# Two ConvFFNs and their surroundings: norms beside the GLU, four products ahead, copies in another room, w_out two tiles behind

## The chip, the cores and the metric

The kernel runs on one core of a Trainium2 chip, as one launch. The metric is the device time in microseconds (us), as the median of three runs. The engines named below are PE (TensorE, the matmul engine), DVE (VectorE), ACT (ScalarE), POOL (GpSimd) and SP (SyncE, which here issues nearly all DMAs; its DMA queue is written SPq). Each engine works through its own list of instructions in order, and waits at semaphores for the others.

## The reference

A backbone block of depth 2 over 1024 latent tokens and 256 context tokens, width 1024. Layer 0 mixes tokens by an S5 state-space layer and a GLU, layer 1 by a matrix-memory LSTM (mLSTM) with four heads. Each is followed by a gated ConvFFN of inner width 2816 (22 tiles of 128). In layer 1 only the latent tokens are carried on.

```python
def _conv_ffn(h, w_in, conv_w, w_out):
    u = _dwconv(h @ w_in, conv_w)                 # 3 taps along the tokens
    a, g = jnp.split(u, 2, axis=-1)
    return (a * jax.nn.silu(g)) @ w_out
...
    y = jax.nn.gelu(...)                          # end of the S5 mixer
    a, g = jnp.split(y @ glu_w + glu_b, 2, axis=-1)
    return a * jax.nn.sigmoid(g)
...
    proj = hf @ w_in                              # mLSTM: q, k, v, o
    ... heads(proj[..., 2 * D:3 * D]), jax.nn.sigmoid(proj[..., 3 * D:])
...
for i in range(2):                                # the block
    x = x + g1 * y_lat;   ctx = ctx + cg1 * y_ctx            # mixer
    x = x + g2 * _conv_ffn(_rmsnorm(x, norm2_g[i]) * (1 + sc2) + sh2, w_in[i], conv[i], w_out[i])
    ctx = ctx + cg2 * _conv_ffn(...)                         # layer 0 only
return _rmsnorm(x, final_g)
```

## The kernel before, in words

Activations lie with channels on the 128 partitions (8 groups k of 128) and tokens along the free axis. Every fp32 operand of a matmul is split into a high and a low part (`split`, L195 on ACT writes the high part, L196 on DVE the low one), and a product is the sum of three matmuls. Weights come by SP's DMAs into raw slots `wr`, are split into a ring of five slots `s`, and are read from there.

The program runs in stages: S5; GLU of the latent tokens (tile `u`, 8 steps m of two halves); GLU of the context (`uc`, L376, 384 matmuls of 256 columns) with norm 2 of layer 0 between; FFN 0 of the latent tokens (`ffn_wide`, L560); its output product; FFN 0 of the context (`ffn_ctx`: `uf` L376, `cacc` L452); mLSTM (v products with the gates L1319, q, k and o products L344); norm 2 of layer 1; FFN 1 (`ffn_wide` again); final norm.

`ffn_wide` does its input product as Strassen's seven products (numbered 1 to 7) per tile f. A product is 12 matmuls of 512 columns into one PSUM tile (`bA`, `bB` or `bC`). The seven need different forms of the normed activations. Products 1 and 2 need only `B11` and `B21`, which are plain splits (`h` or `he`). Products 6, 5, 7 and 4 need sums and differences (`T1` to `T4`, `B22`; L491 to L503, `hl` and `he`), which DVE builds in place and splits. The weights of products 5, 6, 7 and of two others are sums of raw weights (L544), split in the same ring. A copy (L570) keeps product 1 in a room `s13`; in layer 1 that room lies in row 0 of `x`.

A norm (`Norm`) takes squares (ACT L251), adds them up (L254), sums over partitions by one-column matmuls (`columns`, `nps` L271), takes a reciprocal root in some ten to fourteen tiny instructions (`nv`, `ni`, `nt`, `nr`, L204 to L223, on POOL or DVE) and spreads it over partitions by transposes (`spread`, `nps` L286). Then DVE multiplies (`plain`, `nm` L299). Before FFN 0 there are four norms of 256 columns on POOL.

In `ffn_ctx` step f computes `uf` of tile f, then the output product `cacc` of tile f-1, whose `gh` and `gl` come from the convolution and the gate on ACT and DVE (L460 to L465).

From the context GLU on, PE's order is the order in which the code is written (`manual_schedule`). The order on DVE, ACT, POOL and SP is set by a scheduler's estimate.

Of the kernel before, what the change touches and what calls it, by code (L numbers as in the profile page):

```python
# [425 lines left out]
def ffn_ctx(e, ins, x, H, ring, raws, accs, ubank, gp, beside):  # L426
# [6 lines left out]
    prev = None  # L433
    for f in range(FT + 1):
# [19 lines left out]
        if f < FT:
# [11 lines left out]
            prev = [gp.tile([128, 256], F32R, name=f"g{q}") for q in "hl"]  # L466
            split(nc, *prev, ts[1])
# [41 lines left out]
def ffn_wide(e, ins, layer, F, ring, raws, sums, scr, psum, gd, halves, first):

# [20 lines left out]
    def loads(f):  # L531
        for n, (k, m) in {"A11": (0, f), "A21": (0, f + FT), "A12": (4, f), "A22": (4, f + FT)}.items():
# [719 lines left out]
def mlstm(e, ins, x, xpool, npool, wpool, ahead, left, H, T, hpool):  # L1252
# [219 lines left out]
    def in_proj(h, kinds, passes=BOTH, pools=((wp, 2),), tp=tp):  # L1472

        pools = cycle(pools)
        for kind in kinds:
# [6 lines left out]
            for j in range(2):  # L1482
# [3 lines left out]
                for p in passes if kind == "k" else BOTH[1:]:  # L1486
# [352 lines left out]
def tile_hybrid_block(ctx: ExitStack, tc: tile.TileContext, ins, out):  # L1839
# [37 lines left out]
    with ExitStack() as zrc:
        zrp = zrc.enter_context(tc.tile_pool(name="gzr", bufs=2, reuse_waits="tile"))
        z = glu_tokens(e, x, yscr, zl, zc, zrp)
        for m in range(KT):  # L1880
            us = []
            for half in (1, 0):
                u = pu.tile([128, 2, 512], F32, name="u", tag="u")
                mm_halves(nc, [u[:, b] for b in range(2)], half_weights(e, ring, raws, w, m + 8 * half),
                          lambda k, b, part: z[0][part][:, k, 4 * b:4 * b + 4].rearrange("p i c -> p (i c)"))
                us.append(u)
                if m == 0 and half:
                    glu_residual(e, ins, x, zrp, po)
            glu_gate(e, x, m, us, NCH - NCC, 0, sp)
# [23 lines left out]
    def park0(j):  # L1913
        c = LAT0 + 256 * j
        nc.sync.dma_start(xd[0][:, :, 256 * j:256 * j + 256], x[:, :, c:c + 256])

    def plain0(j):
# [327 lines left out]
```

## Time and profile before

| | us |
|---|---|
| median of 3 runs | 3103.88 (3098.01 to 3104.23) |
| profiled execution, its time | 3099.47 |
| its span | 3097.4 |
| PE busy | 2790.1 (90%) |
| DVE busy | 2143.1 (69%) |
| ACT busy | 1409.3 (45%) |
| POOL busy | 341.7 (11%) |

The span is one profiled execution; its own time is 2.07 us above the span. A row of a timeline is: start, duration, engine, line, operation, output from input, count, and in brackets the idle time before it with what released it. Durations of neighbouring matmuls overlap in the record, so the pace is the distance of starts. Times in the text are on the span's axis.

### The profile page before, as it was taken

Reading aid. Unit: us, or ns where it says so; the run is one execution under the profiler, and the core shown is the slowest. Engines: PE = TensorE matmul, PEld = TensorE weight load, DVE = VectorE, ACT = ScalarE, POOL = GpSimd, SP = SyncE. Lnnn points to the kernel's source line nnn. Section 1 sums busy time; section 2 is a strip of 40 time slices with the busy share of each in tenths; the row PEclk is TensorE's granted clock in tenths of the full one; section 3 lists DMA queues with packets and bytes.
Section 4 is the critical chain, followed back from the end, with each engine's and each line's share of the span. In section 5 each row is a group of like instructions: output and inputs, shape, how many; then the busy total and the mean of one; then the engine's idle time right before and its main releaser. Section 6 shows DMA issues by size and latency. Waiting matters only on the chain.

```text
span 3097.4 us, 44668 instructions
## 1 busy us (share of the span) xinstructions
PE 2790.1 (90%) x16336; PEld 2376.3 (77%) x16336; DVE 2143.1 (69%) x4049; ACT 1409.3 (45%) x2579; POOL 341.7 (11%) x523
## 2 busy tenths in 40 slices
PE   4875399988999999999999899999887999999999
PEld 2561067877788887888998899999876788887877
DVE  6789943359777775437774978878777777777352
ACT  5650413246444454335653344545545444445342
POOL 5440000031000000002001121211112000000011
PEclk9885599999999999999999999999998999999999
DMA  8348536142222226446543443343532122226540
GB/s 227 107 89 255 160 73 203 48 130 86 82 82 82 82 91 205 147 146 202 161 119 98 128 147 127 123 136 99 188 92 69 63 81 82 82 82 216 175 150 28
DMA packets 418187, 382.52 MB, mean 123 GB/s; under 512 B 48248, under 2 KB 348064, under 8 KB 415664
## 3 DMA queue, kind: packets, MB, share of 16 engines
q1 hardware_dynamic: 417632, 379.56, 39.5%
q8 instruction: 128, 2.10, 0.3%
q14 instruction: 91, 0.75, 0.1%
q10 hardware_dynamic: 336, 0.12, 0.0%
HBM read 311.44 MB, written 68.16 MB: 123 GB/s over the span
## 4 chain that ended last, share of the span: by engine, by line
PE 70%; DVE 16%; issue 7%; ACT 3%; DMA 2%; POOL 2%; SPq 1%; DVEq 0%; POOLq 0%; ACTq 0%
PE bA L560 16%; PE acc L639 11%; PE bC L560 8%; PE u L344 6%; PE u L376 6%; PE bB L560 4%; PE uf L376 3%; PE u L1319 3%; PE ou L1536 2%; PE py L1213 2%; PE cacc L452 2%; PE po L1536 2%; DVE X L1191 2%; DVE tmp_v L1188 2%; DVE tmp_v L1190 1%
## 5 line engine op out<-in xcount | busy, mean ns | idle before, releaser
L196 DVE TENSOR_TENSOR s<-wr,s 128x512 fp32r<-128x512 f32 x545 | 377.4, 696 | 375.7 <-ACT s L195 371.7
L195 ACT ACTIVATE s<-wr 128x512 fp32r<-128x512 f32 x545 | 341.3, 631 | 640.7 <-PE bA L560 214.6
L560 PE MATMUL bA<-h,s 128*128 128x512 f32 x1056 | 261.4, 402 | 20.6 <-ACT x L570 14.8
L560 PEld LDWEIGHTS bA<-h,s 128*128 128x128 f32 x1056 | 201.9, 192 | 71.4 <-ACT x L570 15.0
L344 PE MATMUL u<-h,wh 128*128 128x258 f32 (+1 forms) x1184 | 231.5, 284 | 4.1 <-DVE s L1501 2.9
L254 POOL TENSOR_TENSOR nacc<-nacc,nsq 128x256 f32<-128x256 f32 (+1 forms) x96 | 85.7, 904 | 1231.3 <-ACT nsq L251 1219.4
L344 PEld LDWEIGHTS u<-h,wh 128*128 128x128 f32 x1184 | 182.7, 190 | 5.1 <-ACT wh L195 4.3
L344 PE MATMUL u<-h,wl 128*128 128x258 f32 (+1 forms) x640 | 152.5, 284 | 4.5 <-DVE wl L196 4.5
L376 PE MATMUL u<-zh,s 128*128 128x512 f32 x512 | 140.4, 395 | 11.9 <-ACT s L195 11.9
L560 PE MATMUL bA<-he,s 128*128 128x512 f32 x528 | 131.8, 399 | 9.0 <-ACT s L195 6.2
L196 DVE TENSOR_TENSOR h<-wr,h 128x512 fp32r<-128x512 f32 x107 | 71.0, 690 | 89.5 <-ACT h L195 84.9
L639 PE MATMUL acc<-h 128*128 128x512 f32 (+1 forms) x564 | 131.4, 373 | 0.0
L560 PE MATMUL bA<-hl,s 128*128 128x512 f32 x528 | 130.5, 395 | 0.0
L560 PE MATMUL bC<-h,s 128*128 128x512 f32 x528 | 128.3, 398 | 0.0
L560 PEld LDWEIGHTS bA<-he,s 128*128 128x128 f32 x528 | 101.0, 192 | 32.7 <-ACT s L195 6.6
L196 DVE TENSOR_TENSOR m<-wr,m 128x512 fp32r<-128x512 f32 x116 | 79.5, 698 | 65.9 <-ACT m L195 64.4
L544 DVE TENSOR_TENSOR wr<-wr 128x512 f32<-128x512 f32 x176 | 121.8, 694 | 2.7
L376 PEld LDWEIGHTS u<-zh,s 128*128 128x128 f32 x512 | 97.2, 191 | 32.4 <-ACT s L195 12.4
L595 DVE SCALAR_TENSOR_TENSOR x<-x,conv 128x1023 f32<-128x1023 f32 x88 | 112.8, 1282 | 13.3 <-ACT x L594 13.3
L155 PE MATMUL ada<-adaw,csil 128*32 128x256 f32 x560 | 70.6, 602 | 56.9 <-DMA adaw<-in_ada_w_dram 56.9
L639 PE MATMUL acc<-s,s 128*128 128x512 f32 x480 | 115.3, 394 | 6.7 <-DVE s L196 4.6
L560 PEld LDWEIGHTS bC<-h,s 128*128 128x128 f32 x528 | 100.1, 190 | 24.5
(519 smaller groups left out, 7269.1 us busy)
## 6 DMA issues: line engine op xcount, KB each, us to landing
wr<-in_ffn_w_in_dram SPq DMA_DIRECT2D x264, 256.0 KB, 3.0
wr<-in_ffn_w_out_dram SPq DMA_DIRECT2D x220, 256.0 KB, 3.1
adaw<-in_ada_w_dram SPq DMA_DIRECT2D x70, 512.0 KB, 5.2
gd<-x SPq DMA_DIRECT2D x44, 512.0 KB, 2.6
wr<-gd SPq DMA_DIRECT2D x88, 256.0 KB, 3.5
wraw<-in_ml_w_in_dram SPq DMA_DIRECT2D x44, 512.0 KB, 4.4
wr<-in_s_glu_w_dram SPq DMA_DIRECT2D x64, 256.0 KB, 2.9
X<-in_ada_w_dram SPq DMA_DIRECT2D x26, 512.0 KB, 4.8
```

The lines of the kernel that those rows point to most:

```text
L155: nc.tensor.matmul(acc[32 * q:32 * q + 32, h * n:h * n + n], lhsT=e.csil[:, k, :], rhs=wt[:, q, :], start=(k == 0 and h == 0), stop=(k == ...
L195: nc.scalar.activation(hi, src, AF.Copy)
L196: nc.vector.tensor_sub(lo, src, f32(hi))
L254: eng.tensor_add(self.acc, self.acc, sq)
L344: nc.tensor.matmul(outs[b], lhsT=w[:, k, :], rhs=rhs(k, b, part), start=i == 0, stop=i == n - 1)
L376: nc.tensor.matmul(o, lhsT=w, rhs=rhs(k, b, part), start=k + i == 0, stop=(k, i) == (KT - 1, 2), skip_group_check=True)
L544: nc.vector.tensor_tensor(R[n, f], R[x, f], R[y, f], op=op)
L560: nc.tensor.matmul(out, lhsT=w[:, k * 128:(k + 1) * 128], rhs=F(part, b, k), start=first and n == 0, stop=n == 11, skip_group_check=True)
L595: nc.vector.scalar_tensor_tensor(t[:, 1:], u[:, i, :-1], cw[0], t[:, 1:], op0=OP.mult, op1=OP.add)
L639: nc.tensor.matmul(out[:, a:a + n], lhsT=w, rhs=g[:, a:a + n], start=k == 0 and i == 0, stop=k == FT - 1 and i == 2, skip_group_check=True)
L1319: nc.tensor.matmul(at[t], lhsT=H[b](hp, k)[:, 1 + 128 * t:129 + 128 * t], rhs=w[wq][:, k % 4], start=k == 0 and j == 0, stop=k == KT - 1 a ...
L1536: nc.tensor.matmul(out, lhsT=w, rhs=r, start=i + j == 0, stop=(i, j) == (len(terms) - 1, 2))
```

## The change

The latent GLU loop now takes the squares of two norms of 512 columns and parks `x` in DRAM, step by step. Their adds and roots are on DVE. `columns` comes after the first half of the first `uc` product, `spread` after the second, and what follows (`plain`, splits, forms) is dealt out six pieces to each further `uc` step. `ffn_wide` starts with products 1 and 2 of tiles 0 and 1 in both layers; the tile-1 loads `A21`, `A22` come after tile 0's sums. `forms_b` begins with `T3` and `T4` of k = 0. In layer 1 `s13` lies in `wr[10]`, `wr[11]`, there are 6 raw slots in place of 8, the third norm's root is on DVE, and its `spread` and `plain` are written after the first two products. `ffn_ctx` does `w_out` two tiles behind. The o product of head 0 for blocks 1 and 2 (96 matmuls, tile `uo`) is moved from the mLSTM to the end of `ffn_ctx`, and its result goes out by the DMA `od<-so`. The pools of one region stand in another order (`ss`, `wr`, then the slots).

```diff
-    prev = None
-    for f in range(FT + 1):
+    prev = deque()
+    for f in range(FT + 2):
...
-        if prev:
+        if f > 1:
...
-                nc.sync.dma_start(t, w_out[(f - 1) * 128:f * 128, q * 512:(q + 1) * 512])
+                nc.sync.dma_start(t, w_out[(f - 2) * 128:(f - 1) * 128, q * 512:(q + 1) * 512])
...
-            gh, gl = prev
+            gh, gl = prev.popleft()
...
-            prev = [gp.tile([128, 256], F32R, name=f"g{q}") for q in "hl"]
+            prev.append([gp.tile([128, 256], F32R, name=f"g{q}", bufs=3) for q in "hl"])
...
+    for fs, ks in (((t3, t4), (0,)), ((t3,), (1, 2, 3)), ((t4,), (1, 2, 3)), ((b22,), range(4))):
+        for k in ks:
+            for f in fs:
+                f(k)
...
-    order = [(p, f) for f in range(first) for p in (1, 2)]
-    for f in range(FT):
-        order += [(1, f)] * (f >= first) + [(4, f - 1), (3, f - 1)] * (f > 0)
-        order += [(5, f), (6, f), (2, f), (7, f)] if f >= first else [(6, f), (5, f), (7, f)]
+    order = [(1, 0), (2, 0), (1, 1), (2, 1), (6, 0), (5, 0), (7, 0), (4, 0), (3, 0), (6, 1), (5, 1), (7, 1)]
+    for f in range(2, FT):
+        order += [(1, f), (4, f - 1), (3, f - 1), (5, f), (6, f), (2, f), (7, f)]
...
+            if f == 0:
+                loads(1, ("A21", "A22"))
+            elif f < FT - 1:
                 loads(f + 1)
...
-                for p in passes if kind == "k" else BOTH[1:]:
+                for p in passes if kind == "k" else BOTH[2:] if kind == "o" and h == 0 else BOTH[1:]:
...
+    ss = wp.tile([128, 2, 512], F32, name="ss")
+    wr = wp.tile([128, 10, 512], F32, name="wr")
     slots = [wp.tile([128, 2, 512], F32R, name=f"s{i}") for i in range(5)]
-    wr = wp.tile([128, 10, 512], F32, name="wr")
-    ss = wp.tile([128, 2, 512], F32, name="ss")
...
-    n0 = [Norm(e, npool, po, x, LAT0 + 256 * b, 256, "C") for b in range(4)]
...
+                n0 = [Norm(e, gn, po, x, LAT0 + 512 * b, 512, "C", nc.vector, nc.vector, nt=1) for b in range(2)]
+        glu_gate(e, x, m, us, NCH - NCC, 0, sp)
+        for n in n0:
+            n.square(m)
+        nc.sync.dma_start(xd[0][:, m], x[:, m, LAT0:LAT0 + SEQ])
...
-                if m in (0, 1, 2, 3):
-                    n0[m].columns()
-                if m in (1, 2, 3, 4):
-                    plain0(m - 1)
-                if m in (1, 2):
-                    n0[m + 1].squares()
-                    park0(m + 1)
+            if m == 0:
+                for n in n0:
+                    n.columns() if half else n.spread()
+        for _ in range(6 if m else 0):
+            next(steps0, None)
...
+    for j in range(2):
+        us = [pu.tile([128, 512], F32, name="uo", tag=t)[:, :256] for t in "CC"]
+        mm_halves(nc, us, half_weights(e, ring, raws, ins["ml_w_in"][0], 24 + j), lambda k, b, part: H1(b + 1)(part, k)[:, 1:257])
+        s = gp.tile([128, 2, 256], F32, name="so")
+        for b in range(2):
+            nc.scalar.activation(s[:, b], us[b], AF.Tanh, scale=0.5)
+        nc.vector.tensor_scalar(s, s, 0.5, 0.5, op0=OP.mult, op1=OP.add)
+        nc.sync.dma_start(e.od[0, :, j, 0:512], s.rearrange("p b n -> p (b n)"))
...
-    n1 = [Norm(e, npool, pu, x, LAT0 + 256 * b, 256, "C", nc.vector if b == 3 else None, nc.vector if b == 3 else None, nt=3) for b in B1]
+    n1 = [Norm(e, npool, pu, x, LAT0 + 256 * b, 256, "C", nc.vector if b == 3 else None, nc.vector if b in (0, 3) else None, nt=3) for b in B1]
...
-    n1[2].spread()
-    plain(2)
...
-           Ring([xf[:, 0:512], xf[:, 512:1024]]), ss[:, 0])
+           Ring([wr[:, 10], wr[:, 11]]), ss[:, 0])
...
-    raws, sums = Ring([wr[:, i] for i in range(8)]), Ring([wr[:, i] for i in range(8, 12)])
+    raws, sums = Ring([wr[:, i] for i in range(6)]), Ring([wr[:, i] for i in range(6, 10)])
...
         if n == 2:
+            n1[2].spread()
+            plain(2)
             n1[3].columns()
```

On PE, at the start of FFN 0, the first products stood like this (`bA`, `bB`, `bC` are the PSUM tiles; products 1, 2, 6, 5, 7 of tile 0, then 1 of tile 1):

```order
L560 MATMUL bA<-he,s_3388 128x512 x12
L560 MATMUL bB<-he,s_3384 128x512 x12
L560 MATMUL bA<-he,s_3385 128x512 x12
L560 MATMUL bC<-he,s_3386 128x512 x12
L560 MATMUL bA<-hl,s_3387 128x512 x12
L560 MATMUL bA<-he,s_3388 128x512 x12
```

and stand now like this:

```order
L567 MATMUL bA<-he,s_3390 128x512 x12
L567 MATMUL bB<-he,s_3386 128x512 x12
L567 MATMUL bA<-he,s_3387 128x512 x12
L567 MATMUL bB<-he,s_3388 128x512 x12
L567 MATMUL bA<-he,s_3389 128x512 x12
L567 MATMUL bC<-he,s_3390 128x512 x12
L567 MATMUL bA<-hl,s_3386 128x512 x12
```

Products 1 and 2 of tile 1 (third and fourth row) stand ahead of product 6 of tile 0, which was third.

On DVE, shortly before that product 6 can be complete, the changed program has these rows (`he<-x` in the last row but one is the low part of the last piece of `T2`, which product 6 reads; `hl` are pieces of other forms):

```order
L504 TENSOR_TENSOR x<-x 128x512
L492 TENSOR_TENSOR x<-x,ss 128x512
L500 TENSOR_TENSOR x<-x 128x512
L196 TENSOR_TENSOR he<-x,he 128x512
L196 TENSOR_TENSOR hl<-x,hl 128x512 x5
L549 TENSOR_TENSOR wr<-wr 128x512
L196 TENSOR_TENSOR hl<-x,hl 128x512 x3
L504 TENSOR_TENSOR x<-x 128x512
L196 TENSOR_TENSOR hl<-x,hl 128x512 x2
L196 TENSOR_TENSOR he<-x,he 128x512
L196 TENSOR_TENSOR hl<-x,hl 128x512
```

Ten `hl` splits stand ahead of that last piece of `T2`.

On SP's DMA queue, from the end of `ffn_ctx` into the mLSTM, the rows before were:

```order
L445 DMA wr<-in_ffn_w_out_dram 128x512 x4
L1338 DMA gb<-in_ml_b_if_dram 128x2x4 x2
L1301 DMA wraw<-in_ml_w_in_dram 128x4x256
L1304 DMA wraw<-in_ml_w_if_dram 128x4x4 x4
L1301 DMA wraw<-in_ml_w_in_dram 128x4x256
L1304 DMA wraw<-in_ml_w_if_dram 128x4x4 x4
```

and are now:

```order
L445 DMA wr<-in_ffn_w_out_dram 128x512 x6
L363 DMA wr<-in_ml_w_in_dram 128x4x128 x4
L1307 DMA wraw<-in_ml_w_in_dram 128x4x256
L1310 DMA wraw<-in_ml_w_if_dram 128x4x4 x2
L2053 DMA od<-so 128x512
L1310 DMA wraw<-in_ml_w_if_dram 128x4x4 x2
L1307 DMA wraw<-in_ml_w_in_dram 128x4x256
L1310 DMA wraw<-in_ml_w_if_dram 128x4x4 x4
```

The store `od<-so` stands between the loads of the first v weights, with six small gate loads and one large load behind it.

## Rows read from the trace of the kernel before

**Rows 1.** Stretches: us, busy and instructions of PE, PEld, DVE, ACT, POOL; PEclk; DMA:

```profile
500.00:550.00 50.00, 50.00 (x261) 42.24 (x260) 15.48 (x23) 14.35 (x24) 0.00 (x0) 1.00 0.40 132
684.00:756.00 72.00, 57.33 (x358) 51.20 (x358) 70.23 (x130) 48.44 (x99) 20.75 (x26) 0.88 0.39 110
1690.00:1760.00 70.00, 63.23 (x521) 61.76 (x520) 66.98 (x118) 23.72 (x33) 10.11 (x7) 0.96 0.30 93
```

**Rows 2.** Waits of PE, 655 to 800 us: total, times, longest:

```profile
PE nps L286 <- POOL nr L223: 8.3, 2, 5.7
```

**Rows 3.** Timeline of PE, context GLU and first products of FFN 0:

```profile
664.31 0.36 PE L376 MATMUL uc<-zh,s 128*128 128x256 f32 x1
...
670.00 0.50 PE L271 MATMUL nps<-ones,nacc 128*128 128x1 f32 x4
...
728.88 2.98 PE L560 MATMUL bB<-he,s 128*128 128x512 f32 x12
738.04 1.22 PE L560 MATMUL bA<-he,s 128*128 128x512 f32 x2 [6.18 <-ACT s L195]
741.56 3.86 PE L560 MATMUL bA<-he,s 128*128 128x512 f32 x10 [2.29 <-DVE s L196]
745.26 1.08 PE L560 MATMUL bC<-he,s 128*128 128x512 f32 x4
```

**Rows 4.** Timeline of DVE, the splits before FFN 0:

```profile
743.83 4.29 DVE L196 TENSOR_TENSOR hl<-x,hl 128x512 fp32r<-128x512 f32 x7
```

**Rows 5.** Waits of PE, 1400 to 1640 us:

```profile
PE cacc L452 <- ACT gh L195: 11.6, 5, 3.1
PE u L1319 <- ACT wh L195: 6.7, 1, 6.7
PE cacc L452 <- DVE gl L196: 3.4, 5, 1.2
```

**Rows 6.** Timeline of PE, context FFN and first v products:

```profile
1425.87 0.38 PE L452 MATMUL cacc<-gl,m 128*128 128x256 f32 x1 [0.71 <-DVE gl L196]
...
1429.80 0.41 PE L452 MATMUL cacc<-gh,m 128*128 128x256 f32 x1
...
1623.62 0.39 PE L452 MATMUL cacc<-gl,s 128*128 128x256 f32 x1 [0.23 <-DVE gl L196]
...
1634.51 0.82 PE L1319 MATMUL u<-wh,h 128*128 128x272 f32 x2 [6.71 <-ACT wh L195]
...
1639.17 0.41 PE L1319 MATMUL u<-wh,h 128*128 128x272 f32 x2
```

**Rows 7.** SP's DMA queue after the last cacc matmul:

```profile
1627.84 0.37 SPq L1301 DMA_DIRECT2D wraw<-in_ml_w_in_dram  x1
1628.25 2.29 SPq L1304 DMA_DIRECT2D wraw<-in_ml_w_if_dram  x4
```

**Rows 8.** DMA issues, 1615 to 1645 us: count, KB, us to landing:

```profile
wraw<-in_ml_w_if_dram SPq DMA_DIRECT2D x8, 8.0 KB, 2.9
```

**Rows 9.** Timeline of ACT, first split of v weights:

```profile
1633.36 1.09 ACT L195 ACTIVATE wh<-wraw 128x1088 fp32r<-128x1088 f32 x1
```

**Rows 10.** Timeline of DVE, start of the mLSTM's gate chain:

```profile
1691.75 0.41 DVE L1399 COPY gi<-pt 4x256 f32<-4x256 f32 x1 [4.94 <-PE pt L1396]
```

**Rows 11.** Timeline of PE, first products of FFN 1:

```profile
2366.47 0.69 PE L286 MATMUL nps<-kc,nr 128*128 128x128 f32 x2 [7.85 <-POOL nr L223]
2366.82 5.47 PE L560 MATMUL bA<-h,s 128*128 128x512 f32 x12
...
2406.44 1.22 PE L560 MATMUL bA<-h,s 128*128 128x512 f32 x2 [0.76 <-DVE h L196]
2407.45 4.16 PE L560 MATMUL bC<-h,s 128*128 128x512 f32 x12
```

**Rows 12.** Timeline of DVE, third norm's root and forms of layer 1:

```profile
2377.47 0.16 DVE L210 SCALAR_TENSOR_TENSOR nt<-nt,nv 128x2 f32<-128x2 f32 x1
...
2381.49 1.26 DVE L299 SCALAR_TENSOR_TENSOR nm<-x,gain,nps 128x256 f32<-128x256 f32 x3 [1.61 <-PE nps L286]
```

More of the change, by code (lines that the diff above doesn't have):

```diff
@@ L529, in half, with loads @@
         return half_of(t, 0, halves[i])
-    def loads(f):
-        for n, (k, m) in {"A11": (0, f), "A21": (0, f + FT), "A12": (4, f), "A22": (4, f + FT)}.items():
+    def loads(f, names=("A11", "A21", "A12", "A22")):
+        for n in names:
+            k, m = 4 * (n[2] == "2"), f + FT * (n[1] == "2")
             R[n, f] = raws()
@@ L600, in gated @@
         nc.sync.dma_start(gd[f], tg)
-    for f in range(first):
-        loads(f)
+    loads(0)
+    loads(1, ("A11", "A12"))
     ahead = len(ring.items)
-    late = 2 * first if first > 1 else 0
     for n in range(ahead - 1):
@@ L611, in ffn_wide @@
         yield n
-        if n == late:
-            for i in order[:late]:
+        if n == 4:
+            for i in order[:4]:
                 combine(*i)
         product(p, f)
-        if n >= late:
+        if n >= 4:
             combine(p, f)
@@ L1875, in tile_hybrid_block @@
     halves = (0, 1), (2, 3)
-    n0 = [Norm(e, npool, po, x, LAT0 + 256 * b, 256, "C") for b in range(4)]
[L1877 to L1889, printed above, removed]
+    zrc = ExitStack()
+    zrp = zrc.enter_context(tc.tile_pool(name="gzr", bufs=2, reuse_waits="tile"))
+    z = glu_tokens(e, x, yscr, zl, zc, zrp)
+    for m in range(KT):
+        us = []
+        for half in (1, 0):
+            u = pu.tile([128, 2, 512], F32, name="u", tag="u")
+            mm_halves(nc, [u[:, b] for b in range(2)], half_weights(e, ring, raws, w, m + 8 * half),
+                      lambda k, b, part: z[0][part][:, k, 4 * b:4 * b + 4].rearrange("p i c -> p (i c)"))
+            us.append(u)
+            if m == 0 and half:
+                glu_residual(e, ins, x, zrp, po)
+                zrc.close()
+                gn = gc.enter_context(tc.tile_pool(name="gn", bufs=1, side="right", reuse_waits="tile"))
+                n0 = [Norm(e, gn, po, x, LAT0 + 512 * b, 512, "C", nc.vector, nc.vector, nt=1) for b in range(2)]
[3 more added lines that the diff above has]
+        nc.sync.dma_start(xd[0][:, m], x[:, m, LAT0:LAT0 + SEQ])
     lc.close()
@@ L1911, in blocks0, with steps0 @@
         return half_of(x, k * NCOL + LAT0, halves[i])
[L1913 to L1917, printed above, removed]
-        c = LAT0 + 256 * j
-        n0[j].spread()
-        n0[j].plain(lambda k: x[:, k, c:c + 256], 0, 1)
-        if j == 1:
-            for k in range(4):
-                for f, kk in ((B11, k), (B21, k + 4)):
-                    split(nc, two(F0(0, f, k)), two(F0(1, f, k)), blocks0(kk, 0))
+    def steps0():
+        for j in range(2):
+            c = LAT0 + 512 * j
+            for k in range(KT):
+                n0[j].plain(lambda k: x[:, k, c:c + 512], 0, 1, (k,))
+                yield
+                if not j and k > 3:
+                    for f, kk in ((B11, k - 4), (B21, k)):
+                        split(nc, two(F0(0, f, k - 4)), two(F0(1, f, k - 4)), blocks0(kk, 0))
+                        yield
+        for k in range(4):
+            forms_a(nc, F0, k, blocks0(k, 0), blocks0(k, 1), blocks0(k + 4, 1), two(ss[:, k % 2]))
+            for _ in range(4):
+                yield
+    steps0 = steps0()
     order = ExitStack()
     order.enter_context(tc.manual_schedule(engines={nc.tensor.engine}))
-    for j in range(2):
-        n0[j].squares()
-        park0(j)
     for m in range(KT):
@@ L1969, in tile_hybrid_block @@
     load, mm, add = ffn_out(e, ins, 0, x, gd[0], ring, raws)
-    for n in ffn_wide(e, ins, 0, F0, ring, raws, sums, scr, bank0, gd[0], halves, 1):
+    for n in ffn_wide(e, ins, 0, F0, ring, raws, sums, scr, bank0, gd[0], halves):
         if n == 10:
```

31 lines of the change are left out of this document (15 added, 16 removed).

## The prediction, made blind

> **What bounds the kernel now.** I read the page first: PE is busy 90% of the span, so a gain must come from the places where PE stands. The table of stretches of 50 us shows those places, the list of PE's waits names them, and the timelines of PE, DVE and SP tell what came last. Four places matter for this change.
>
> First, the context GLU and the start of FFN 0. PE waits for roots on POOL [rows 2], and then for DVE: from 684 to 756 us DVE is busy 70.23 of 72 us while PE is busy 57.33 [rows 1]. Product 6 waits 6.18 and 2.29 us, and product 5 begins at 745.26 with only three products behind it [rows 3]. Second, the context FFN: `cacc` waits 11.6 us for `gh` and 3.4 for `gl`, in five places each [rows 5]. Third, the step into the mLSTM: after the last `cacc` matmul SP issues the v weights at 1627.84 and PE is at its pace again at 1639.17 [rows 6, 7]. Fourth, the start of FFN 1: 7.85 us for a root on POOL, then a DVE chain from 2381.49 to the last wait of product 6 at 2406.44 [rows 11, 12]. During the latent GLU, by contrast, PE is full and DVE is busy 15.48 of 50 us [rows 1].
>
> **Latent GLU: norms and parking.** Added per step are two squares on ACT, two adds on DVE (512 columns, 0.61 each, from seven splits in 4.29 us [rows 4]) and one store. DVE and ACT have over 34 us in 50 free there [rows 1], and PE works from a ring of five slots. I cost it at nothing; if that cover fails it is the slow rival below.
>
> **Context GLU and first products, layer 0.** `columns` still ends when it did, at 664.3 [rows 3]. The two roots are then 24 tiny DVE instructions. One is busy 0.16 [rows 12]; I take 0.2 from start to start, an estimate, and one split between: `spread` at 669.7. The POOL wait of 5.7 us [rows 2] goes. What is late next is DVE. In its new order, from the first `nm` to the last `T2` piece, there stand 107 instructions of about 0.61 us (16 `nm` of 512 columns, which have no row and are priced as splits of that width, 59 splits, 16 steps of the forms, 8 weight sums, 8 gate products) and 9 short ones, at an estimate of 0.4: 65.3 + 3.6 = 68.9. That puts the last `T2` piece at 738.6; with 1.4 for waits I take 740. PE meanwhile has 336 `uc` matmuls at 0.1185 (48 of them between 664.31 and 670.00 [rows 3]), 39.8 us, and four products of 2.8 (12 matmuls, bB in 2.98 with its tail [rows 3]), and is ready for product 6 by about 721. So product 5 begins at 740 + 1.0 (the same two matmuls took 1.0 in layer 1, 2406.44 to 2407.45 [rows 11]) = 741 with five products behind it, against 745.3 with three: 4.3 + 2 x 2.8 = 9.9. Product 5 itself comes out of a long wait. In layer 1, after such a wait, it took 4.16 [rows 11] against 2.8, so 1.4 is given back: 8.5 us. Lower bound: the ten `hl` splits and the sums hold `T2` until 745, which leaves 3.5. Upper bound: the ten `hl` splits fall into waits, 6.1 earlier, 15.
>
> The change gathers several short waits into one long one, and the mean granted clock of 684 to 756 was 0.88 [rows 1], a mix of the levels 1.2 and 2.4 GHz. The Trainium skill ("TensorE: Matmul & The Clock Gate", Part 1: The HAM clock gate) says that the throttled state is the default and activity releases it, which speaks against gathering the waits. The 4.16 of layer 1 agrees. By the rule product 7 could be slow too, and the gain then 7.1 instead of 8.5.
>
> **Context FFN, `w_out` two tiles behind.** Before, one `cacc` of 24 and one `uf` of 48 matmuls lie between the end of `uf(f)` and `cacc(f)`: 72 x 0.1185 = 8.5 us. Now it is twice that, 17. The waits are at most 3.1 and 1.2 us long [rows 5], so the chain through convolution, gate and split needs up to about 12.5, and is covered. Of 15.0 us of waits the last place (3.1 + 0.2) belongs to the next part: 11.7. After a wait `cacc` runs slower: the 22 intervals from 1425.87 to 1429.80 took 3.93 [rows 6] against 2.6 at 0.1185, so 1.3 more at each of four places. Together 16.9. I take 14.5, as DVE and ACT stay as full as they were and the weight splits, now earlier against the gates, can come last once or twice. Bounds 8 and 17. A third `g` buffer keeps the writer from waiting.
>
> **Into the mLSTM.** Before, the loss is 3.3 for the last `gh`/`gl`, 1.5 for slow matmuls (1623.62 to the end at 1627.8, 4.2 instead of 2.7), and 1627.8 to 1639.17 less the 12 matmuls done in it, 11.4 - 1.6 = 9.8: 14.6 in all [rows 6]. Now `cacc` is followed by 96 matmuls `uo`, 11.4 us, and the v weights no longer share a room with the slots, so the first large load goes out early. But the store `od<-so` stands in SP's order ahead of two of the first half's gate loads and of the whole second half. It waits for the first half of `uo`: 5.7 + about 1.3 for tanh and scaling (estimate) = 7.0 after the last `cacc`. Then two gate loads at 0.57 (four in 2.29 [rows 7]), 2.9 to land [rows 8], 1.1 for the split [rows 9]: 12.2, against PE's 11.4. The second half comes after another 0.4 + 2.3 of issuing: 14.9, where PE would want it at 13.7. With the low parts behind the high ones the residue is about 3, and 0.5 for the clock: gain 14.6 - 3.5 = 11. Bounds: no residue, 14.6; all eight small loads and one more split late, 6, so 8.6.
>
> The Trainium skill ("DMA: Bandwidth & Descriptors", Anatomy of one DMA) says that DMA engines do not wait on semaphores, the issuing sequencer does, before dispatch. That speaks against this store in this queue. Rows 7, where the gate loads go out one by one behind the first load, agree with an ordered queue. Were the store not in the way the gain would be 14, by the rule it is the 11 above.
>
> **The o product's move.** It costs 11.4 us before the mLSTM and saves 11.4 inside, if PE's work is what bounds there. From 1690 to 1760 DVE is busy 66.98 of 70 us [rows 1], so PE's work would be worth nothing there, unless that DVE chain starts earlier too. It does: DVE stood idle 4.94 us for the transposes `pt` [rows 10], and in PE's order 99 matmuls of L344 stand ahead of these, 192 before: 93 fewer, 11.0 us. So I take 0; bounds -11.4 (chain held by its inputs) and +3 (two more loads of weights and their splits now lie in a covered place).
>
> **Layer 1.** The third norm's nm no longer stand between the plain splits in DVE's queue, where DVE stood until the root on POOL came [rows 11]. Product 1 of tile 0 then runs with the splits (it took 5.47 at a slow clock [rows 11]), and the four products end about 5 us earlier. The fourth norm's root now queues behind a weight split, so its `spread` moves from 2381.1 to about 2377.5 (estimate): 3.6. The chain of DVE from there to the last `T2` piece was 25.0 us [rows 11, 12]; two instructions fewer, 1.2. Sum 4.8, say 5; bounds 1 (the queue is full anyhow) and 10. `s13` in another room frees ACT's copies, but DVE's chain ends last there, so that is worth nothing by itself.
>
> **Sum.** 8.5 + 14.5 + 11 + 0 + 5 = 39. The profiled execution took 3099.47 (span 3097.4 and 2.07 around it), so it would take 3060.5. The median lies 4.4 above that execution, so 3065.
>
> **Rivals.**
> A, DVE binds: DVE and ACT set both FFN starts, and fewer waits of PE only lengthen others. For: 70.23 of 72. Against: the roots on POOL left DVE idle too. Layer 0 gives 3.5, layer 1 gives 1: 3074.
> B, the o product is not given back: the gate chain's inputs come no earlier. For: DVE's 66.98 of 70. Against: the 4.94 idle for PE. 11.4 worse: 3076.
> C, the change does not do what it says in the context FFN: the waits are named for `gh`, but weight splits queued on ACT and DVE end just behind, and two tiles of lag only move the wait to them. 14.5 less: 3080.
> D, nearly all idle goes: 15 + 17 + 14.6 + 10 + 3 = 60: 3044.
> E, slower: the adds of the two norms wait on DVE for squares, which wait for each step's gate, and weight splits queue behind them. If that held DVE for longer than four of the five slots last (24 matmuls of 512 columns, 5.6 us each, so 22 us), PE would lose up to a slot per step: 8 x 5.6 = 45, so 3110. Against: DVE's idle time in the GLU [rows 1].
>
> **How the numbers follow.** Forecast 0.42, A 0.20, B 0.15, C 0.08, D 0.10, E 0.05. The lower bounds of all parts together are 3.5 + 8 + 8.6 - 11.4 + 1 = 10, so 3094; the upper ones are D's, 3044. That is the range. About 0.2% (6.2 us) is what a measurement can tell from no change. Faster than that is every case but E and two of A, B, C together at their worst: 0.88; the same 0.07; slower 0.05.
>
> **What would show it.** Right: no wait of `cacc` for `gh` before the last tile; `uo` following `cacc` at once and a wait of 2 to 4 us at the first v products, the `od` store on SP just ahead of gate loads; `spread` at about 670 and product 5 of tile 0 near 741; in layer 1 product 5 near 2402.5 on the old axis. Wrong: PE gaps in the latent GLU, `cacc` waiting for `m` or `s` splits, a PE wait in the early mLSTM longer by 5 us or more than before, or DVE waiting at a root.

## The result and the profile after

The changed kernel takes **3058.73 us** (median of 4 runs, 3057.70 to 3059.88) against 3103.43 for the kernel before on the same chip: ratio 0.986, 95% interval 0.9843 to 0.9877. The forecast was 3065 within 3044 to 3094. The profiled execution has a span of 3055.9 us, 41.5 less than before.

The traces are cut here at the same landmarks of PE's timeline: the first `uc` matmul (context GLU), the first `uf` (context FFN), the end of the last `cacc`, the first v product that reads `g` (PE is at its pace in the mLSTM), the end of the last `ou` matmul, and product 5 of tile 0 of FFN 1 (the first that writes `bC`). Every time is the difference between two landmarks, in us:

| kernel | to `uc` | GLU, FFN 0 | context FFN | step | mLSTM | layer 1 start | rest | span |
|---|---|---|---|---|---|---|---|---|
| before | 658.1 | 752.6 | 217.1 | 23.9 | 706.4 | 49.4 | 690.0 | 3097.4 |
| after | 656.4 | 747.5 | 195.8 | 29.7 | 691.2 | 44.6 | 690.6 | 3055.9 |
| e1 | 657.7 | 747.8 | 215.2 | 29.9 | 695.2 | 45.5 | 690.7 | 3081.9 |
| e2 | 659.1 | 745.9 | 195.8 | 23.2 | 701.9 | 44.6 | 690.0 | 3060.6 |
| e3 | 658.3 | 745.7 | 195.8 | 31.7 | 691.8 | 44.6 | 691.3 | 3059.3 |
| e4 | 656.4 | 747.5 | 195.8 | 28.3 | 690.9 | 45.0 | 691.7 | 3055.6 |
| e5 | 657.0 | 748.4 | 195.8 | 31.8 | 691.4 | 44.6 | 689.4 | 3058.6 |
| e6 | 656.6 | 748.5 | 195.8 | 31.9 | 692.6 | 44.6 | 690.8 | 3060.9 |
| e7 | 657.7 | 750.5 | 195.8 | 29.9 | 691.7 | 44.6 | 691.0 | 3061.2 |
| e8 | 659.0 | 747.8 | 195.8 | 30.0 | 694.4 | 50.6 | 689.4 | 3067.0 |
| e9 | 657.3 | 741.6 | 195.8 | 29.6 | 694.9 | 38.7 | 690.1 | 3048.1 |
| e9b | 658.0 | 738.7 | 195.9 | 31.9 | 693.6 | 35.0 | 696.3 | 3049.4 |
| e10 | 657.6 | 752.3 | 195.8 | 32.3 | 695.0 | 45.7 | 690.9 | 3069.7 |
| e11 | 657.2 | 741.3 | 195.8 | 28.3 | 696.7 | 38.7 | 692.4 | 3050.4 |

The columns also show what one execution is worth. Where no edit touches a stage, the context FFN repeats within 0.1 us, but "GLU, FFN 0" ranges from 745.7 to 750.5, the step stands at 30 or at 32, and the mLSTM ranges from 690.9 to 696.7. Much of this is TensorE's clock. Windows (columns as in [rows 1]) of the step, after and e3:

```profile
1599.74:1629.42 29.68, 27.16 (x212) 26.01 (x211) 17.10 (x41) 11.41 (x24) 1.05 (x19) 1.00 0.35 90
1599.83:1631.57 31.74, 28.68 (x212) 27.52 (x212) 17.06 (x41) 11.35 (x24) 1.05 (x19) 0.95 0.41 101
```

The granted clock is 1.00 in every step of about 30 (after, e1, e7, e8, e9) and 0.95 in every one of about 32 (e3, e5, e6, e9b, e10): most of the 2 us are a short stretch at the lower of the clock's two levels, 1.2 GHz. FFN 0 has such a stretch too. PE's timeline of the same product, behind the same wait for a root of 2.6 us, first after, then in e5:

```profile
777.84 4.59 PE L567 MATMUL bA<-he,s 128*128 128x512 f32 x12
781.02 2.98 PE L570 MATMUL bA<-he,s 128*128 128x512 f32 x12
```

The granted clock is 0.57 from 778 to 782 after and 1.00 from 781 to 785 in e5; e7 has one more stretch (0.50 from 1159.7 to 1166.5). In the mLSTM the clock explains a part only (0.99 in e3, 0.97 in e11). Why it falls in one execution and not in another stays open.

For FFN 0 the first product of tile 2 is a better landmark: the same twelve products stand ahead of it in every order. It begins 112.0 us behind the first `uc` before and 107.0 after; 105.2 to 107.3 in the kernels that leave the stage alone (e1 to e4, e7, e8); 109.5 in e5, 107.9 in e6, 113.4 in e10 and 101.1 in e9.

So after against before the gains are 21.3 (context FFN), 5.1 (FFN 0, with 1.7 in what lies before it), 9.4 (step and mLSTM together) and 4.8 (layer 1).

Windows of the trace after: the latent GLU, the start of FFN 0, and the part of it until the last `T2` piece:

```profile
500.00:550.00 50.00, 50.00 (x259) 42.21 (x258) 15.87 (x23) 12.95 (x23) 0.00 (x0) 1.00 0.42 136
684.00:756.00 72.00, 56.97 (x341) 49.37 (x341) 65.26 (x109) 44.09 (x81) 6.28 (x6) 0.88 0.34 97
684.00:742.00 58.00, 43.93 (x290) 39.26 (x290) 58.00 (x99) 39.30 (x74) 6.28 (x6) 0.87 0.39 111
```

The latent GLU is as full as in [rows 1]: PE has no gap. From 684 to 742 DVE is busy all of 58 us. The timeline of PE, after, answers to [rows 3]:

```profile
662.37 3.48 PE L271 MATMUL nps<-ones,nacc 128*128 128x1 f32 x16 [3.03 <-DVE nacc L254]
670.24 1.03 PE L286 MATMUL nps<-kc,nr 128*128 128x128 f32 x8
...
718.86 2.88 PE L567 MATMUL bB<-he,s 128*128 128x512 f32 x12
722.77 1.19 PE L567 MATMUL bA<-he,s 128*128 128x512 f32 x4 [1.03 <-ACT x L577]
727.24 1.56 PE L567 MATMUL bA<-he,s 128*128 128x512 f32 x3 [3.27 <-DVE he L196]
732.39 1.65 PE L567 MATMUL bA<-he,s 128*128 128x512 f32 x3 [3.59 <-DVE he L196]
740.22 1.22 PE L567 MATMUL bA<-he,s 128*128 128x512 f32 x2 [6.18 <-DVE he L196]
741.24 4.38 PE L567 MATMUL bC<-he,s 128*128 128x512 f32 x12
...
749.38 3.05 PE L567 MATMUL bA<-hl,s 128*128 128x512 f32 x12 [0.96 <-ACT x L586]
```

The four products of two tiles stand before the waits, and product 5 begins at 741.24. Product 6 reads the four `T2` factors as they come, and waits 3.27, 3.59 and 6.18 us for them. DVE's timeline, after, shows what the longest of these waits was behind:

```profile
732.24 3.10 DVE L196 TENSOR_TENSOR hl<-x,hl 128x512 fp32r<-128x512 f32 x5
735.25 0.69 DVE L549 TENSOR_TENSOR wr<-wr 128x512 f32<-128x512 f32 x1
735.86 1.89 DVE L196 TENSOR_TENSOR hl<-x,hl 128x512 fp32r<-128x512 f32 x3
737.66 0.69 DVE L504 TENSOR_TENSOR x<-x 128x512 f32<-128x512 f32 x1
738.26 1.29 DVE L196 TENSOR_TENSOR hl<-x,hl 128x512 fp32r<-128x512 f32 x2
739.47 0.69 DVE L196 TENSOR_TENSOR he<-x,he 128x512 fp32r<-128x512 f32 x1
```

The last `he` piece ends at 740.16. Ten `hl` splits stand ahead of it, and product 7, the first to read them (`bA<-hl`), comes a whole product later. So they are early where `T2` is late.

PE's waits from 1380 to 1640 us, after:

```profile
PE u L1325 <- DVE wl L196: 1.6, 2, 0.8
PE nps L286 <- POOL nr L223: 0.8, 1, 0.8
PE u L1325 <- ACT wh L195: 0.5, 1, 0.5
```

No `cacc` wait is left of the 15.0 us in [rows 5]. SP's DMA queue there, after (start, us to issue; answers to [rows 7]):

```profile
1593.92 0.37 SPq L1307 DMA_DIRECT2D wraw<-in_ml_w_in_dram  x1
1594.34 1.05 SPq L1310 DMA_DIRECT2D wraw<-in_ml_w_if_dram  x2
1606.54 0.34 SPq L2053 DMA_DIRECT2D od<-so  x1
1606.92 1.12 SPq L1310 DMA_DIRECT2D wraw<-in_ml_w_if_dram  x2
1608.09 1.12 SPq L1307 DMA_DIRECT2D wraw<-in_ml_w_in_dram  x1
1609.25 2.57 SPq L1310 DMA_DIRECT2D wraw<-in_ml_w_if_dram  x4
```

The queue stands for 11 us, and as soon as `od<-so` goes out the two gate loads behind it follow. ACT's first split of v weights, after, waits for these loads:

```profile
1610.83 1.11 ACT L195 ACTIVATE wh<-wraw 128x1088 fp32r<-128x1088 f32 x1 [4.47 <-DMA wraw<-in_ml_w_if_dram]
```

PE, after, goes from `uo` to the v products with hardly a gap:

```profile
1605.83 6.13 PE L376 MATMUL uo<-h,m 128*128 128x256 f32 x48 [0.36 <-ACT so L2051]
1612.00 0.52 PE L1325 MATMUL u<-wh,h 128*128 128x272 f32 x2
1613.33 0.40 PE L1325 MATMUL u<-wl,h 128*128 128x272 f32 x1 [0.81 <-DVE wl L196]
```

In layer 1 the wait for a root of 7.85 us [rows 11] has become two short ones (PE's timeline, after):

```profile
2332.28 0.43 PE L286 MATMUL nps<-kc,nr 128*128 128x128 f32 x2 [0.75 <-DVE nr L211]
...
2340.02 0.43 PE L286 MATMUL nps<-kc,nr 128*128 128x128 f32 x2 [1.29 <-DVE nr L211]
...
2364.27 1.22 PE L567 MATMUL bA<-h,s 128*128 128x512 f32 x2 [0.76 <-DVE h L196]
2365.29 4.72 PE L567 MATMUL bC<-h,s 128*128 128x512 f32 x12
```

### The profile page after: what moved, and what is told of

It reads as the page before. It is cut to its first block, busy times and chain, and to the rows that moved or that the text cites. A ratio compares the mean times of both kernels' runs of the same rounds, so it can differ in the third digit from the quotient of the medians.

```text
span 3055.9 us, 44585 instructions
## 1 busy us (share of the span) xinstructions
PE 2781.0 (91%) x16336; PEld 2366.1 (77%) x16336; DVE 2145.8 (70%) x4068; ACT 1402.8 (46%) x2553; POOL 301.7 (10%) x449
## 4 chain that ended last, share of the span: by engine, by line
PE 75%; DVE 16%; ACT 3%; DMA 2%; issue 2%; POOL 1%; SPq 1%; DVEq 0%; ACTq 0%; POOLq 0%
PE bA L567 15%; PE acc L645 15%; PE bC L567 8%; PE u L344 6%; PE u L376 6%; PE bB L567 4%; PE uf L376 3%; PE u L1325 3%; PE ou L1542 2%; PE py L1219 2%; PE po L1542 2%; PE cacc L452 2%; DVE X L1197 2%; DVE tmp_v L1194 2%; PE uc L376 1%
## 5 line engine op out<-in xcount | busy, mean ns | idle before, releaser
L344 PE MATMUL u<-h,wh 128*128 128x258 f32 (+1 forms) x1120 | 221.9, 285 | 2.7 <-DVE s L1507 1.6
L254 POOL TENSOR_TENSOR nacc<-nacc,nsq 128x256 f32<-128x256 f32 (+1 forms) x72 | 63.7, 895 | 1260.3 <-ACT nsq L251 1255.4
L344 PEld LDWEIGHTS u<-h,wh 128*128 128x128 f32 x1120 | 174.6, 191 | 3.5 <-issue 3.4
L344 PE MATMUL u<-h,wl 128*128 128x258 f32 (+1 forms) x608 | 145.9, 285 | 3.0 <-DVE wl L196 3.0
L376 PEld LDWEIGHTS u<-zh,s 128*128 128x128 f32 x512 | 96.5, 189 | 31.8 <-ACT s L195 12.1
```

Of the source, the lines that this page charges most:

```text
L254: eng.tensor_add(self.acc, self.acc, sq)
L344: nc.tensor.matmul(outs[b], lhsT=w[:, k, :], rhs=rhs(k, b, part), start=i == 0, stop=i == n - 1)
L376: nc.tensor.matmul(o, lhsT=w, rhs=rhs(k, b, part), start=k + i == 0, stop=(k, i) == (KT - 1, 2), skip_group_check=True)
```

## The experiments

Each kernel is the changed one with an edit or two more. Ratios are to the kernel before on the same chip; since that kernel took from 3098.6 to 3103.9 us there, totals are compared by ratio.

**e1, `w_out` one tile behind again.** The tile that is loaded and the first and last step of the sum follow.

```diff
-    for f in range(FT + 2):
+    for f in range(FT + 1):
...
-        if f > 1:
+        if f > 0:
...
```

> The changed kernel with the context FFN's w_out one tile behind again, nothing else undone. Theory of the prediction: the chain through convolution, gate and split needs up to 12.5 us and one tile covers 8.5, so the waits of cacc for gh and gl come back, about 11.7 us and 5 us of slow matmuls in the middle and about 4 at the last tile: some 20 us more, 3075 to 3080. Rival: the weight splits on ACT and DVE end just behind the gates, so the lag was worth little: within 5 us of 3059.

3083.07 us (0.9947, 0.9932 to 0.9962). The context FFN goes from 195.8 to 215.2, which is 19.4 of the 21.3 us, and PE's waits in e1 from 1380 to 1640 us are those of [rows 5] again:

```profile
PE cacc L452 <- ACT gh L195: 10.1, 5, 2.4
PE cacc L452 <- DVE gl L196: 3.0, 4, 1.0
```

So the second tile of lag is the cause. Weight splits do not take the place of the wait, and rival C is out. Of the 26.0 us that the span loses, 4.0 more lie in the mLSTM, where nothing was edited; that is within its range.

**e2, the o product back inside the mLSTM.** The block of `uo` at the end of `ffn_ctx` is dropped, with its store.

```diff
-                for p in passes if kind == "k" else BOTH[2:] if kind == "o" and h == 0 else BOTH[1:]:
+                for p in passes if kind == "k" else BOTH[1:]:
```

> The changed kernel with the o product of head 0, blocks 1 and 2, back inside the mLSTM and without the store od<-so. Theory: what removes the wait at the step into the mLSTM is that the v weights have a room of their own and are loaded early; the o product only costs and gives back the same 11.4 us, so within 4 us of 3059, with 1 to 2 us of waiting at the first v products. Rival: the o product is the cover of that step, and without it a wait of 8 us or more returns: 3067 or more.

3062.88 us (0.9879, 0.9862 to 0.9895). The step is 6.5 shorter and the mLSTM 10.7 longer: the 11.4 us of matmuls are given back almost whole. The reason stands on DVE. In e2 the gate chain begins like this (DVE's timeline):

```profile
1664.11 0.41 DVE L1405 COPY gi<-pt 4x256 f32<-4x256 f32 x1 [4.95 <-PE pt L1402]
```

and after like this:

```profile
1659.65 0.40 DVE L1405 COPY gi<-pt 4x256 f32<-4x256 f32 x1
```

From the first product that reads `g` (1624.03 in e2, 1629.42 after) that is 40.1 against 30.2 us, and the idle 4.95, which [rows 10] show too, is gone. The step alone gains only 6.5 from dropping 11.4 us of work, since without this cover the first v product waits (PE's waits in e2, 1595 to 1800 us):

```profile
PE u L1325 <- ACT wh L195: 5.5, 1, 5.5
```

The expected wait of 1 to 2 us was too short: the room of the v weights does not remove the wait, the cover does.

**e3, the pools in the old order**, so that the v weights lie in a room that the slots used last.

```diff
-    ss = wp.tile([128, 2, 512], F32, name="ss")
-    wr = wp.tile([128, 10, 512], F32, name="wr")
     slots = [wp.tile([128, 2, 512], F32R, name=f"s{i}") for i in range(5)]
+    wr = wp.tile([128, 10, 512], F32, name="wr")
+    ss = wp.tile([128, 2, 512], F32, name="ss")
```

> The changed kernel with the three tiles of the weight pool in the old order (slots, wr, ss), so that the mLSTM's v weights share a room with the slots again. Theory: the first v load then waits for PE's last read of a slot in the o product, and its 3 us of landing and 1.1 of split lie open: the wait at the first v products grows from 2.5 to about 9, so 3065. Rival: the loads have to wait for the store in SP's queue anyway, so the room is worth nothing: within 2 us of 3059.

3060.94 us (0.9872, 0.9857 to 0.9887): not told apart from after. SP's first large load of v weights goes out at 1602.80 instead of 1593.92, and the step is 2 us longer, which goes with its granted clock of 0.95 instead of 1.00. The 3065 that was expected did not come. Nine us earlier is worth so little because the gate loads that the split needs stand behind the `od` store in either kernel.

**e4, the store `od<-so` in ACT's queue.**

```diff
-        nc.sync.dma_start(e.od[0, :, j, 0:512], ...)
+        nc.scalar.dma_start(e.od[0, :, j, 0:512], ...)
```

> The changed kernel with the two stores od<-so issued by ACT instead of SP. Theory: the store holds back the gate loads behind it in SP's queue, which are what the first v split waits for (4.5 us on ACT); without it the gate loads go out by 1597 and the waits of 1.6 and 0.5 us at the first v products shrink to under 1: 1 to 2 us less, 3057. Rival: the splits and the low parts set that wait, not the loads: no change.

3057.74 us (0.9861, 0.9846 to 0.9876). All loads of v weights are out by 1600.4 and the step takes 28.3 us, the shortest of the kernels that have `uo` in it; e11, with the same edit, has 28.3 too, and the others without a stretch at the lower clock 29.6 to 30.0. So the store does delay the gate loads, but it costs 1.4 us, less than the total times can tell.

**e5, FFN 0 with one tile ahead.** Tile 0's products 1, 2, 6, 5, 7 come first, as before. Product 2 of tile 1 is multiplied by weights of tile 2 here; no size changes.

```diff
-    order = [(1, 0), (2, 0), (1, 1), (2, 1), (6, 0), (5, 0), (7, 0), ...
+    order = [(1, 0), (2, 0), (6, 0), (5, 0), (7, 0), (1, 1), (4, 0), ...
```

> The changed kernel with FFN 0's products in the order of before: products 1 and 2 of tile 0, then 6, 5, 7 of tile 0, products of tile 1 after that; FFN 1 as changed. Theory: DVE sets the time of product 6 (busy 58.00 of 58 us up to it), two weight splits fewer stand ahead of it (1.2 us), and two products of 2.8 us are no longer done in the wait: 4 us more, 3063. Rival: DVE is full for so long after product 6 that it paces PE anyway and the two products' lead is lost again: no change.

3064.03 us (0.9881, 0.9866 to 0.9896). Product 5 is where it was, now with three products behind it (PE's timeline):

```profile
739.69 1.22 PE L570 MATMUL bA<-he,s 128*128 128x512 f32 x2 [5.78 <-DVE he L196]
740.71 3.81 PE L570 MATMUL bC<-he,s 128*128 128x512 f32 x12
```

Two products fewer should cost 5.6. At the first product of tile 2 it is 2.5: product 5 begins 83.7 us behind the first `uc` (after: 84.9), takes 3.6 us and not 4.2, and product 4 no longer waits the 0.96 that it does after. The stage as a whole shows 0.9, as the stretch at the lower clock that after has at 778 is missing here. The total is 0.21% above after, with intervals that overlap.

**e6, the norms of the context GLU as before** (four of 256 columns, roots on POOL, `x` parked beside the `uc` steps), two tiles ahead kept.

```diff
-                n0 = [Norm(e, gn, po, x, LAT0 + 512 * b, 512, "C", nc.vector, nc.vector, nt=1) for b in range(2)]
+    n0 = [Norm(e, npool, po, x, LAT0 + 256 * b, 256, "C") for b in range(4)]
```

> The changed kernel with the GLU section of before: four norms of 256 columns with adds and roots on POOL, columns and spread between the context products, parking in four stores at the end of the GLU; the four products ahead stay. Theory, DVE binds: PE's waits for POOL (8.3 us) and for DVE between the context products return, but they are hidden behind DVE's queue, which is about as long as now, so product 5 of tile 0 begins 1 to 5 us later: 3060 to 3064. Rival, the roots on POOL were what cost: 10 us or more come back, 3069 or more.

3065.05 us (0.9885, 0.987 to 0.9899). The roots on POOL cost PE 7.0 us again (after: 2.6) and `nm` 4.6, but product 5 begins at 742.64, 86.0 after the first `uc` against 84.9. This stage shows only 1.0, and 0.9 at the first product of tile 2, which is inside the scatter there. The total is 0.25% above after, again with intervals that overlap, and a little above the 3060 to 3064 expected.

**e10, both undone**: e6's norms and e5's order, with the tile-1 loads where they stood.

> The changed kernel with both parts ahead of FFN 0 undone: the GLU section of before and the order of FFN 0's products of before; FFN 1, context FFN and mLSTM as changed. Each part undone alone cost 1 us between the first context product and the first product of the context FFN (747.5 us; 748.4 and 748.5 without one of them; 752.6 before). Theory: the two do the same job, each lets PE do other work while DVE builds T2, so undoing both costs the whole 5: 752 to 753 for that stretch, 3062 to 3065 in all. Rival: the rest comes from the new order of the forms (T4 of k = 0 ahead), which stays: 749 to 750.

3072.27 us (0.9914, 0.9899 to 0.9929). Here the stage takes 752.3, as before (752.6), and product 6 waits as in [rows 3] (PE's timeline):

```profile
737.41 1.22 PE L570 MATMUL bA<-he,s 128*128 128x512 f32 x2 [6.20 <-ACT s L195]
740.92 4.63 PE L570 MATMUL bA<-he,s 128*128 128x512 f32 x10 [2.29 <-DVE s L196]
745.35 3.66 PE L570 MATMUL bC<-he,s 128*128 128x512 f32 x12
```

So the two parts are worth 4.8 us together in this stage, and the new order of the forms, which stays here, adds nothing that shows. Whether either part alone would bring most of the gain is not shown. At the first product of tile 2 e5 loses 2.5, e6 0.9 and e10 6.4, but kernels that leave the stage alone differ by 2.1 there; and by the totals the losses add up, 0.21 and 0.25% for the parts and 0.54% (17 us) for both, more than the 3062 to 3065 expected. Of this about 2 us lie in the step, whose granted clock is 0.95 in e5, e6 and e10, and up to 4 in the mLSTM, within its range.

**e7, the room of `s13` in layer 1 as before.**

```diff
-           Ring([wr[:, 10], wr[:, 11]]), ss[:, 0])
+           Ring([xf[:, 0:512], xf[:, 512:1024]]), ss[:, 0])
```

> The changed kernel with the room of s13 in layer 1 back in row 0 of x. Theory: ACT's copies then wait until the forms have read that row, and PE's bank with them (14.8 us by name before), but product 6 ends with the last piece of T2 from DVE either way: within 2 us of 3059, though the wait is named for the copy again. Rival: that wait is real, and 5 us or more come back.

3059.32 us (0.9864, 0.9848 to 0.9881); layer 1's start takes 44.6 as after. The waits there (e7, 2300 to 2420 us) look quite different, however:

```profile
PE bA L567 <- ACT x L577: 14.8, 1, 14.8
PE bA L567 <- DVE h L196: 4.7, 3, 3.3
```

After has 11.0 for `h` on DVE and 9.2 for `h` on ACT. One wait of 14.8 us came and nothing was lost, since the last piece of DVE's chain arrives when it did.

**e8, the third norm's `spread` and `plain` before product 1 again.**

```diff
+    n1[2].spread()
+    plain(2)
     next(tail)
```

> The changed kernel with spread and plain of layer 1's third norm written before the first product again (root still on DVE). Theory: PE waits for that root before product 1, and DVE's forms start later: 3 to 5 us more, 3063. Rival: with the root on DVE the wait is short and the chain on DVE is full anyhow: within 1.5 us of 3059.

3067.65 us (0.9892, 0.9878 to 0.9907). Layer 1's start takes 50.6, against 49.4 before. PE's timeline in e8 shows the stall of [rows 11] again, though the root is now on DVE:

```profile
2337.08 0.69 PE L286 MATMUL nps<-kc,nr 128*128 128x128 f32 x2 [9.52 <-DVE nr L211]
2337.42 5.12 PE L567 MATMUL bA<-h,s 128*128 128x512 f32 x12
```

So the engine of the root alone gains nothing; the place of `spread` does. The place with the root still on POOL was not run. The total is above the 3063 expected.

**e9, `T2` ahead of the `hl` splits.** The forms that are not needed yet (`forms_b`) may issue only after the last `T2` piece's copy on ACT, in both layers.

```diff
...
-    forms_b(nc, F0, blocks0)
+    with tc.issue_after(t2_last[0].ins):
+        forms_b(nc, F0, blocks0)
...
```

> The changed kernel with one edit in both layers: the splits of T3, T4 and B22 are queued on ACT behind the high part of the last piece of T2 (issue order only). Theory: DVE's queue sets product 6, and the ten hl splits that stood ahead of that piece are 6 us of it; product 5 of tile 0 then begins about 6 us earlier in layer 0, and PE keeps what DVE can follow of it (DVE had 6.7 us idle in the 14 us after): 3 to 6 us less there, a few more in layer 1, 3050 to 3055. Rival: DVE is full, the work only moves, and products 7 and 4 wait for it: within 2 us of 3058.

3049.68 us (0.9844, 0.9828 to 0.9861). Both FFN starts lose 5.9 us (741.6 and 38.7). Of the three waits of product 6 the last is gone (PE's timeline in e9; 3.59 and 6.18 stand there after):

```profile
733.16 1.65 PE L568 MATMUL bA<-he,s 128*128 128x512 f32 x3 [3.51 <-DVE he L196]
734.97 1.22 PE L568 MATMUL bA<-he,s 128*128 128x512 f32 x2 [0.16 <-DVE he L196]
735.99 4.71 PE L568 MATMUL bC<-he,s 128*128 128x512 f32 x12
```

The `hl` splits in front of `T2` were thus the last of the three waits: product 5 begins 78.6 us behind the first `uc`, against 84.9 (83.1 to 84.9 in the kernels that leave the stage alone). The gain is shown by the two stages and not by the total, which is 0.16% (5 us) below after with intervals that overlap; 3.7 us stand against it in the mLSTM, within its range.

**e9b, the same with DVE held too** (`issue_after` for both instructions of the last `T2` split).

> As the run before, but on DVE too: all of T3, T4 and B22, their subtractions also, stand behind the low part of the last piece of T2. Theory: the queue is then in the order of need (T2, T1, T3, T4, B22), and product 6 can end some 11 us earlier in both layers; part of that is lost again at products 7 and 4, whose pieces come at 1.2 us per 0.7 us of product: 5 to 12 us less than 3058 in all. Rival: all of it is lost at products 7 and 4: no change.

3049.58 us (0.9843, 0.9828 to 0.9857). FFN 0 shows 2.9 more (1.3 at the first product of tile 2, inside the scatter) and layer 1's start 3.7 more, but the rest is 5.7 longer than after. In layer 1 the factors that were put off are now late for product 7, and product 4 waits 2.94 until ACT has copied that out (0.97 in e9; PE's timeline in e9b):

```profile
2359.85 0.97 PE L568 MATMUL bA<-h,s 128*128 128x512 f32 x3 [2.60 <-DVE h L196]
...
2366.53 5.49 PE L568 MATMUL bA<-h,s 128*128 128x512 f32 x12 [2.94 <-ACT wr L587]
```

Product 3, the next, begins 18.7 us behind product 5 there, and 11.0 in e9. A landmark that comes earlier is not yet a gain.

**e11, the best of these**: e9b in layer 0, e9 in layer 1, e4's store.

> The changed kernel with three edits together: in layer 0 all of T3, T4 and B22 queued behind the last piece of T2 on ACT and DVE (that stage 747.5 to 738.8 us when done alone), in layer 1 on ACT only (6.4 us less with what follows), and od<-so issued by ACT (1.2 us). Theory: the three stages do not overlap, so the gains add: 16 us less than the changed kernel, 3042 to 3045 against 3058.7, a ratio of about 0.981 to before. Rival: the mLSTM's start moves by some us with whatever lies ahead of it and takes part of this back: 3047 to 3050.

3052.22 us over 5 rounds (0.9829, 0.9814 to 0.9845). By the ratio it is the fastest kernel measured, 0.3% below after, though the two intervals touch. Its stages show why it is not more: FFN 0 (741.3), the step (28.3) and layer 1 (38.7) keep their gains, 13.5 us in sum, while the mLSTM takes 696.7 (after: 691.2) and the rest 1.8 more. e9b's 2.9 in FFN 0 do not show either (741.3, where e9 has 741.6). The ratio of 0.981 that was expected is not reached, and e11 and e9 cannot be told apart.

## Why the prediction came out

**Latent GLU, costed at nothing: right.** PE is busy 50.00 of 50 us, and rival E never came near.

**FFN 0, 8.5 forecast, 5.1 measured.** Place and cause were right: last `T2` piece at 740 forecast and 740.16 measured, product 5 at 741 and 741.24, DVE without a gap. That the axis agrees so well is luck: the run reached `uc` 1.7 earlier, and counted from there product 5 gained 2.3, not 4.3 (up to 4.0 in the kernels that leave the stage alone). That is one reason why the term was too large. The other is that product 4, which now follows product 7 in the same `bA`, waits 0.96 until ACT has copied that out (`ACT x L586`), which I had not seen. The slow product 5 was as reckoned, 4.21 (741.24 to 745.45). That leaves 2.3 + 5.6 - 1.4 - 1.0 = 5.5. Product 7 took 2.97, with a granted clock of 1.00 from 745.4 on. So the lower gain that I put beside the sum by the Trainium skill's rule ("TensorE: Matmul & The Clock Gate", Part 1: The HAM clock gate) did not come. The ten `hl` splits, which I had in the lower bound, are what is left to gain, as e9 showed.

**Context FFN, 14.5 and 4.8 for the last place, which I had put into the next part: 19.3. Measured 21.3**, of which e1 undoes 19.4. Right, and in both its parts: the 15.0 us of waits are gone, and the stage's granted clock went from 0.97 to 1.00, which is worth about 6.5 of its 217.1 us.

**Step.** Of the 9.8 lost before, 29.7 - (23.9 - 9.8 + 11.4) = 4.2 is left; 3.5 was forecast. (The stretch before holds 15 matmuls and not the 12 that I took off, which makes it 9.5 and 3.9.) SP's order did what was said, with the store ahead of two gate loads, 6.8 us after the last `cacc` where I had 7.0, and the first half's split ended as `uo` did. The named waits are only 2.5 (1.6 for `wl`, 0.5 for `wh` and 0.4 inside `uo`); the rest is not slow matmuls, for which I had put 0.5, as the step's granted clock is 1.00. The queue stood until the store went, while the same loads are out by 1600.4 in e4: this is the rule on the issuing sequencer that I drew from the Trainium skill ("DMA: Bandwidth & Descriptors", Anatomy of one DMA), with 1.4 us as its price where I had reckoned 3. The early room of the v weights is worth 2 at most, and these go with the clock (e3).

**The o product, 0 forecast within -11.4 to +3: +3.8** (11.4 more in the step, 15.2 less in the mLSTM). By e2 it is -0.7: the mLSTM gets 10.7 longer for 11.4 of matmuls, and the rest of what e2 loses is the missing cover, which the sum has under the step. Both are within the mLSTM's own spread of 5.8, so the sign is not settled. That DVE's chain would start as much earlier as PE's queue is shorter, 11.0 us, came nearly true: 40.1 to 30.2, 9.9. Rival B is out.

**Layer 1, 5 forecast, 4.8 measured, and by the steps given.** The last `spread` stands 19.4 us after the last `ou` (23.0 before), 3.6 forecast and found; the chain from it to the last wait is 24.3 instead of 25.3. The room of `s13` was worth nothing, as said (e7). The place of `spread` carries this (e8). Rival A is out as a whole, but its mechanism, DVE's queue, is what e9 shortened.

**Sum.** 39 forecast, 41.5 measured on the span. It came out closer than its terms: the 3.4 too much in FFN 0 stands against 3.8 at the o product, 2.0 in the context FFN and 1.7 ahead of the first `uc`, where nothing was forecast. That these cancel is luck. Of the 6.3 us between 3065 and the result the larger part, 3.4, comes from the offset: I added the 4.4 by which the median lay above the execution profiled before, as if it belonged to the kernel, and after it is 1.0 (3057.7 to 3058.73).

## What to carry to other kernels

Put a second tile between producer and consumer where the same wait comes back step after step; it was the largest and surest gain here and is read straight from the list of waits. Where an engine is full and others wait for it, look at the order in which it works and not at the total: what is needed last stood ahead of what is needed first, and turning that round (e9) gave 5.9 us in each FFN start, as much as the whole edit of FFN 0. Before you read a difference of 1 or 2 us in a stage, look at the granted clock of that stage in both traces: here a short stretch at the lower level was most of what made a step of 30 us one of 32.

## What was not expected of the hardware

After a long wait a product of 12 matmuls took 4.38 us (after, layer 0), 4.72 (after, layer 1) and 5.12 (e8, layer 1), against 2.88 at pace. The granted clock after was 1.00 from 720 to 727 and 0.50, the lower level of 1.2 GHz, from 727.5 to 744.4: it fell while product 6 waited for its pieces and rose again while product 5 ran without a gap. In layer 0 of e9b product 6 waits 10.09 us in one piece, by name for ACT's copy, and then finds all of `T2` there; it is slow itself, and product 5 runs at pace (PE's timeline):

```profile
731.92 5.47 PE L568 MATMUL bA<-he,s 128*128 128x512 f32 x12 [10.09 <-ACT x L578]
737.21 2.92 PE L568 MATMUL bC<-he,s 128*128 128x512 f32 x12
```

Several short waits inside a product cost a slow product behind it, as in after; one long wait costs one slow product too.

A wait in the list need not be a loss: in e7 one of 14.8 us appeared and the stage did not change.
